# Norm and combination of the second half's first three row blocks moved ahead of the last block

## The chip, the cores and the metric

The kernel runs on one core of a Trainium2 chip. The metric is the device time of one launch in microseconds. PE is TensorE, DVE is VectorE, ACT is ScalarE, POOL is GpSimd, and SP is the engine that issues the DMAs spoken of here.

## What is computed

One decoder layer on x of 1024 rows and 1024 columns in float32: a gated recurrent branch and a sparse attention branch, merged by gates, an output projection with a residual, a norm, and a squared-ReLU MLP with a residual. The change lies between the output projection and the first products of the MLP:

```python
def rms_norm(x, g):
    xf = x.astype(jnp.float32)
    y = xf * lax.rsqrt(jnp.mean(xf * xf, axis=-1, keepdims=True) + EPS)
    return (y * g.astype(jnp.float32)).astype(x.dtype)
...
    merged = jax.nn.sigmoid(gate_a) * o_gdn + jax.nn.sigmoid(gate_b) * o_att
    x = x + merged @ w_out
    h2 = rms_norm(x, norm_mlp_g)
    x = x + jnp.square(jax.nn.relu(h2 @ w_mlp_up)) @ w_mlp_down
    return x
```

## The kernel before

**Tiles.** The 1024 rows are eight row blocks of 128 rows (qb 0 to 7). Blocks 0 to 3 are the first half, 4 to 7 the second. The attention units and the output projection `wout` go through the blocks in the order 0, 7, 1, 6, 2, 3, 5, 4, each with two units (g of 0 and 1), so block 4 is the last. Behind a block's second unit, `residual` (line 1397) adds the two PSUM banks `dd` to the residual rows x1 (the tiles w0 to w7: block 0 is in w3, 1 in w2, 2 in w6, 3 in w7, 4 in w4, 5 in w0, 6 in w5, 7 in w1), stores them by SP, and sums the squares on ACT (`th,nss<-w`). `wout` starts a block's first unit only when the residual of the block ahead has emptied both banks.

**First half.** `norm2` (line 1424) waits for the sums of squares of all four blocks, finds the inverse roots nr by a Newton iteration (`rsq_w`, line 101: with the first scaling, eleven operations of DVE on 128x4 numbers, each of which needs the one ahead of it), scales the rows on DVE and transposes them on PE into banks of two rings, `s` and `pt`, of two banks each. Each bank is evacuated by ACT (rounded part, `ha`) and then by DVE (the rest, `la`), and only then is it free again. The MLP's up-products (`dd<-ha,m`, `o<-la,m`) are computed by a scheme that multiplies sums and differences of the two halves' column halves; the first products need the first half alone.

**Second half.** `norm2b` (line 1587) waits for the sums of squares of all four blocks, makes one Newton iteration for them, scales the four blocks' second column halves (`hh<-w,nr`, y22), and passes five combinations of rows through `columns` (line 1633), one after another: set 0 (y22), set 2, set 3, set 1 and set 4. A set is sixteen transposes in four banks, with an evacuation of 128x512 by ACT (`hh`) and one by DVE (`hl`) for each bank; four operations of DVE on 128x512 (one for each block) make the rows of the next set.

**Order.** A planner (`Weave`, from line 2003) runs all these generators as chains with priorities when the program is built. It emits, at each moment of its own clock, the next step of the ready chain with the lowest number. It holds a price for each operation; a DVE operation costs 0.07 us and 1/960 us for each element of a partition. A step is what a generator emits between two `yield`s. The resulting order of each engine is fixed in the program; on the chip each engine takes its own list strictly in order and waits where an operand isn't there yet. `rsq_w` yields between its operations, so in the kernel before other operations of DVE may be emitted between them.

## Time and profile before

| | |
|---|---|
| median of 3 runs | 1824.97 us (1824.21 to 1825.02) |
| the profiled execution's own time | 1824.57 us |
| its span in the trace | 1822.9 us |
| granted TensorE clock | 1.00 |
| PE busy | 1807.4 us (99%) |
| DVE, ACT, POOL busy | 1266.2, 1036.2, 525.5 us |
| output projection ends, first MLP products begin | at about 1195 us of the span |
| the second half's sets are made | from about 1200 to 1250 us |

The times in the rows below count from the start of the span. A row of the timeline gives its start, its length, the engine, the line of the helper that records it, the operation, output and inputs, how many alike stand in it, and in brackets how long the engine was idle ahead of it and which engine it waited for. An operation's length overlaps the next one's start, so the pace of a run of operations is read from start to start. PE has next to no idle time, so the few places where it has some are what a reordering can win or lose.

### The profile page before, as it was taken

To read this page: it belongs to the slowest core of one execution; us is meant where nothing else is said; L and a number is where in the kernel's file an instruction comes from. 1 tells how busy PE (TensorE), PEld (TensorE's weight loads), DVE (VectorE), ACT (ScalarE), POOL (GpSimd) and SP (SyncE) were. 2 spreads that over 40 slices of the span, in tenths; PEclk is the share of its full clock that TensorE was granted. 3 is DMA by queue.
4 is the path that set the end of the run, shared out by engine and by line. 5 is a ranking of instruction groups with operands and counts; after the bars stand their busy time and mean duration, and the time that the engine had idled before them with its cause. 6 is when DMAs were issued, how large, how long until landed. Compare 5 with 4: busy or idle time off the path is not lost. (4 is left out here: it accounts for less than half of the span.)

```text
span 1822.9 us, 28546 instructions
## 1 busy us (share of the span) xinstructions
PE 1807.4 (99%) x10316; PEld 1542.0 (85%) x10316; DVE 1266.2 (69%) x2626; ACT 1036.2 (57%) x2273; POOL 525.5 (29%) x738
## 2 busy tenths in 40 slices
PE   9999999999999999999999999999999999999999
PEld 8999998888888888888887888887888888888887
DVE  5556768857777869764448767687766668969673
ACT  6566657765776545445337656576676664343331
POOL 0003530733461724245013111221323322222230
PEclk9999999999999999999999999999999999999999
DMA  4111242132222222231356222224535459473331
GB/s 163 48 47 47 71 128 64 49 97 76 57 58 54 78 70 62 69 84 35 98 168 208 89 77 74 73 89 149 195 136 165 147 173 347 149 249 126 102 133 55
DMA packets 192192, 198.80 MB, mean 109 GB/s; under 512 B 36737, under 2 KB 140466, under 8 KB 192050
## 3 DMA queue, kind: packets, MB, share of 16 engines
q1 hardware_dynamic: 192050, 196.97, 34.2%
q8 instruction: 81, 1.33, 0.3%
q14 instruction: 61, 0.50, 0.1%
HBM read 141.20 MB, written 55.74 MB: 108 GB/s over the span
## 5 line engine op out<-in xcount | busy, mean ns | idle before, releaser
L2114 PE MATMUL dd<-hh,w 128*128 128x512 f32 x1568 | 518.0, 402 | 0.0
L2114 PEld LDWEIGHTS dd<-hh,w 128*128 128x128 f32 x1568 | 288.2, 189 | 50.6
L2114 PE MATMUL dd<-hl,w 128*128 128x512 f32 x784 | 316.1, 403 | 0.9 <-DVE hl L2114 0.9
L2114 ACT ACTIVATE m<-m 128x512 fp32r<-128x512 f32 (+1 forms) x240 | 139.9, 625 | 80.1 <-PE o L2114 30.5
L2114 PE MATMUL dd<-w,hh 128*128 128x256 f32 x960 | 179.4, 284 | 0.4 <-DVE w L2114 0.4
L2114 PE MATMUL dd<-hh,m 128*128 128x512 f32 x520 | 172.1, 396 | 1.0 <-DVE w L2114 0.8
L2114 PEld LDWEIGHTS dd<-hl,w 128*128 128x128 f32 x784 | 147.8, 189 | 26.6 <-DVE hl L2114 1.4
L2114 DVE TENSOR_TENSOR m<-m,m 128x512 fp32r<-128x512 f32 (+2 forms) x184 | 139.4, 784 | 40.8 <-ACT m L2114 35.5
L2114 PEld LDWEIGHTS dd<-w,hh 128*128 128x128 f32 x960 | 151.5, 191 | 1.5 <-DVE w L2114 0.6
L2114 PE MATMUL dd<-w,hl 128*128 128x256 f32 x480 | 136.2, 284 | 0.0
L2114 POOL TENSOR_TENSOR sx<-sx,stmp 128x60 f32<-128x60 f32 (+24 forms) x248 | 110.1, 444 | 19.4
L2114 PEld LDWEIGHTS dd<-hh,m 128*128 128x128 f32 x520 | 96.7, 188 | 20.6 <-DVE w L2114 2.4
L2114 DVE TENSOR_SCALAR_CACHE_REDUCE tkeq<-sc,cand 128x384 f16<-128x384 f32 (+3 forms) x128 | 103.3, 807 | 1.1
L2114 POOL TENSOR_TENSOR m<-m,m 128x512 f32<-128x512 f32 x48 | 67.9, 1421 | 123.5 <-ACT m L2114 60.3
L2114 PE MATMUL dd<-hl,m 128*128 128x512 f32 x260 | 102.3, 393 | 0.9 <-POOL hl L2114 0.9
L2114 POOL TENSOR_TENSOR stmp<-sx,um 128x60 f32<-128x60 f32 (+24 forms) x186 | 79.2, 426 | 64.7 <-DMA um<-ZA 51.1
L2114 ACT ACTIVATE hh<-m 128x1024 fp32r<-128x1024 f32 x44 | 45.2, 1056 | 88.7 <-PE s L2114 41.5
L2114 ACT ACTIVATE ha<-m 128x1024 fp32r<-128x1024 f32 x44 | 45.4, 1056 | 87.7 <-PE s L2114 34.1
L2114 PEld LDWEIGHTS dd<-w,hl 128*128 128x128 f32 x480 | 91.7, 191 | 0.6
L2114 DVE TENSOR_TENSOR w<-w,w 128x1024 fp32r<-128x1024 f32 (+1 forms) x60 | 67.6, 1130 | 33.4 <-ACT w L2114 32.8
L2114 ACT ACTIVATE tkcm<-sc,cand 128x896 f16<-128x896 f32 x64 | 69.9, 1091 | 25.7 <-DVE cand L2114 22.1
L2114 PE MATMUL o<-hh,m 128*128 128x512 f32 x248 | 80.2, 391 | 0.0
(412 smaller groups left out, 4435.4 us busy)
## 6 DMA issues: line engine op xcount, KB each, us to landing
HD<-m SPq DMA_DIRECT2D x112, 256.0 KB, 2.5
m<-HD SPq DMA_DIRECT2D x56, 512.0 KB, 3.9
w<-in_w_in_dram SPq DMA_DIRECT2D x48, 512.0 KB, 3.9
m<-in_w_mlp_up_dram SPq DMA_DIRECT2D x33, 512.0 KB, 5.2
wraw<-in_w_in_dram SPq DMA_DIRECT2D x8, 1024.0 KB, 5.2
m<-in_w_mlp_down_dram SPq DMA_DIRECT2D x16, 512.0 KB, 6.8
w<-in_x_dram SPq DMA_DIRECT2D x10, 512.0 KB, 4.5
es<-GC SPq DMA_DIRECT2D x8, 512.0 KB, 4.6
```

The source lines that it names most:

```text
L2114: ins = f(*args, **kw)
```

## The change

The residuals get priority -1 instead of 1. `rsq_w` can emit a whole Newton iteration in one step (`apart=False`), and the new `roots` always does so. The first half's norm is made in two parts, blocks 0 to 2 and then block 3, each with its own Newton iteration; half of the scalings go to ACT; its priority falls from 2 to 8. For the second half a new chain `early` makes the roots of blocks 6 and 7 (one iteration) and of block 5 (another), the scaled rows and the combinations of these three blocks; `early_columns` transposes three blocks' columns of the sets 0 and 2 into three quarters of the banks and evacuates 128x384. `norm2b` is left with block 4 (a fifth iteration): `last_columns` transposes four columns of it into one bank for each of the two sets and evacuates the bank in two parts of 128x2x128. The sets 3, 1 and 4 are made for all four blocks as before. The number of matmuls and transposes is the same.

```diff
@@ -98,15 +98,19 @@
     wv = Weave(tc)
     V_, A_, G_, PE_, SY_ = (wv.engine(e, n) for e, n in ((V, "V"), (A, "A"), (G, "G"), (PE, "PE"), (SY, "SY")))
-    def rsq_w(pl, dst, src, n, tag):
-        t = pl.tile([P, n], F32, name=tag + "t")
+    def rsq_w(pl, dst, src, n, tag, apart=True):
+        t = pl.tile([P, max(n, 4)], F32, name=tag + "t")[:, :n]
         V_.tensor_scalar(dst.bitcast(I32), src.bitcast(I32), -0.5, float(0x5F3759DF), op0=OP.mult, op1=OP.add)
         for _ in range(3):
-            yield
+            if apart:
+                yield
             V_.scalar_tensor_tensor(t, dst, -0.5, src, op0=OP.mult, op1=OP.mult)
-            yield
+            if apart:
+                yield
             V_.tensor_tensor(t, t, dst, op=OP.mult)
-            yield
+            if apart:
+                yield
             V_.scalar_tensor_tensor(dst, t, 1.5, dst, op0=OP.add, op1=OP.mult)
     units = ([("misc", [(0, C_GA, 16), (16, C_IK, 72)])]
@@ -1391,7 +1395,7 @@
                         yield 0.0
             wv.done("wo", idx)
             if g:
-                wv.add(1, residual(qb, pw))
+                wv.add(-1, residual(qb, pw))
         wv.done("wout")
     def residual(qb, pw):
@@ -1420,22 +1424,31 @@
         yield
         wv.done("h2k", half, k)
+    def roots(tbs):
+        for tb in tbs:
+            yield ("ss", tb)
+        bs = slice(min(tbs), max(tbs) + 1)
+        V_.tensor_scalar(nms[:, bs], nss[:, bs], 1.0 / D, EPS, op0=OP.mult, op1=OP.add)
+        yield from rsq_w(cst, nr[:, bs], nms[:, bs], len(tbs), "n2", apart=False)
+        yield
     def norm2():
-        for tb in range(4):
-            yield ("ss", first * 4 + tb)
-        bs = slice(first * 4, first * 4 + 4)
-        V_.tensor_scalar(nms[:, bs], nss[:, bs], 1.0 / D, EPS, op0=OP.mult, op1=OP.add)
-        yield
-        yield from rsq_w(cst, nr[:, bs], nms[:, bs], 4, "n2")
-        yield
-        for tb in range(4):
-            yield ("xd", first * 4 + tb)
+        tbs = [qb for qb, g in ATT if g and qb // 4 == first]
+        for now in (tbs[:3], tbs[3:]):
+            yield from roots(now)
+            for tb in now:
+                yield ("xd", tb)
+                for c, eng in enumerate("VA"):
+                    yc = x1[tb][:, c * HALF:(c + 1) * HALF]
+                    yield eng
+                    if c:
+                        A_.activation(yc, yc, AF.Copy, scale=nr[:, tb:tb + 1])
+                    else:
+                        V_.tensor_scalar(yc, yc, nr[:, tb:tb + 1], None, op0=OP.mult)
+        yield
         for c in range(2):
             ys = [x1[first * 4 + i][:, c * HALF:(c + 1) * HALF] for i in range(4)]
-            for i in range(4):
-                V_.tensor_scalar(ys[i], ys[i], nr[:, first * 4 + i:first * 4 + i + 1], None, op0=OP.mult)
-            yield
             for k in range(4 * c, 4 * c + 4):
                 ring = (ss, ptr)[k % 2]
                 yield ring.ready
@@ -1443,6 +1456,72 @@
                 for i in range(4):
                     PE_.transpose(ps[:, i * P:(i + 1) * P], ys[i][:, (k % 4) * P:(k % 4 + 1) * P], ident)
                 wv.add(1, norm_out(first, k, ps, ring, slot_))
+            yield
+            wv.done("turned", c)
+    part = lambda h, c: [x1[4 * h + i][:, c * HALF:(c + 1) * HALF] for i in range(4)]
+    y22, comb, pairs = {}, {}, {}
+    places = {0: 0, 2: 2, 3: 4, 1: 6}
+    def early(tbs):
+        yield from roots(tbs)
+        for tb in tbs:
+            i, r = tb % 4, nr[:, tb:tb + 1]
+            b11, b12 = part(first, 0)[i], part(1 - first, 0)[i]
+            y22[i] = part(1 - first, 1)[i]
+            yield ("xd", tb)
+            yield "A"
+            A_.activation(y22[i], y22[i], AF.Copy, scale=r)
+            yield
+            yield ("turned", 0)
+            yield "V"
+            V_.scalar_tensor_tensor(b11, b12, r, b11, op0=OP.mult, op1=OP.subtract)
+            yield "V"
+            V_.scalar_tensor_tensor(b12, b12, r, y22[i], op0=OP.mult, op1=OP.subtract)
+            yield
+            wv.done("combined", i)
+    def early_columns():
+        js = [tb % 4 for tb in EARLIER]
+        for j in js:
+            yield ("combined", j)
+        yield ("wo", NA - 2)
+        for m in (0, 2):
+            if m:
+                yield
+                for j in js:
+                    yield "V"
+                    V_.tensor_tensor(y22[j], y22[j], part(first, 0)[j], op=OP.subtract)
+                yield
+            for k in range(4):
+                if k % 2 == 0:
+                    pairs[m, k // 2] = [hpair(f"{n}{places[m] + k // 2}") for n in ("hh", "hl")]
+                    for i in range(2):
+                        comb[m, k + i] = [t[:, i] for t in pairs[m, k // 2]]
+                ring = (ss, ptr)[k % 2]
+                yield ring.ready
+                ps, slot_ = ring.get()
+                for j in js:
+                    PE_.transpose(ps[:, j * P:(j + 1) * P], y22[j][:, k * P:(k + 1) * P], ident)
+                wv.add(2, early_rounded(m, k, ps, ring, slot_))
+        yield
+        wv.done("early")
+    def early_rounded(m, k, ps, ring, slot_):
+        cs = slice(min(EARLIER) % 4 * P, (max(EARLIER) % 4 + 1) * P)
+        hi, lo = (t[:, cs] for t in comb[m, k])
+        yield 0.2
+        yield "A"
+        A_.activation(hi, ps[:, cs], AF.Copy)
+        yield
+        yield "V"
+        V_.tensor_tensor(lo, ps[:, cs], hi.bitcast(F32), op=OP.subtract)
+        ring.free(slot_)
+    EARLIER = sorted(qb for qb, g in ATT[:-1] if not g and qb // 4 != first and qb != ATT[-1][0])
     wv.add(1, kprep())
     wv.add(0, loadq())
@@ -1478,7 +1557,10 @@
             h2h[2 * j + i, first], h2l[2 * j + i, first] = th[:, i, :], tl[:, i, :]
     wv.run(until=("pv", NA - 2))
-    wv.add(2, norm2())
+    wv.add(8, norm2())
+    for tbs in (EARLIER[1:], EARLIER[:1]):
+        wv.add(2, early(tbs))
+    wv.add(2, early_columns())
     NP = FF // (2 * P)
@@ -1580,55 +1662,50 @@
         if p == UP[-1]:
             wv.done("rfree", q)
-    comb = {}
     def norm2b():
-        half = 1 - first
-        for tb in range(4):
-            yield ("ss", half * 4 + tb)
-        bs = slice(half * 4, half * 4 + 4)
-        V_.tensor_scalar(nms[:, bs], nss[:, bs], 1.0 / D, EPS, op0=OP.mult, op1=OP.add)
-        yield
-        yield from rsq_w(cst, nr[:, bs], nms[:, bs], 4, "n2")
-        yield
-        yt = [hpair(n, F32) for n in ("hh6", "hh7")]
-        y22 = [yt[i // 2][:, i % 2] for i in range(4)]
-        for i in range(4):
-            tb = half * 4 + i
-            o, src, r = y22[i], x1[tb][:, HALF:], nr[:, tb:tb + 1]
-            if i % 2:
-                A_.activation(o, src, AF.Copy, scale=r)
-            else:
-                V_.tensor_scalar(o, src, r, None, op0=OP.mult)
-        wv.add(0, columns(0, y22))
-        yield
-        part = lambda h, c: [x1[4 * h + i][:, c * HALF:(c + 1) * HALF] for i in range(4)]
-        t1, t4, t3, t2 = part(first, 0), part(first, 1), part(half, 0), part(half, 1)
+        tb = ATT[-1][0]
+        i, r = tb % 4, nr[:, tb:tb + 1]
+        yield from roots([tb])
+        y = hpair("hh6", F32)[:, 0]
+        t1, t4, t3, t2 = part(first, 0), part(first, 1), part(1 - first, 0), part(1 - first, 1)
+        V_.tensor_scalar(y, t2[i], r, None, op0=OP.mult)
+        yield
+        yield ("early",)
+        wv.add(0, last_columns(0, i, y))
+        V_.scalar_tensor_tensor(t1[i], t3[i], r, t1[i], op0=OP.mult, op1=OP.subtract)
         yield ("T", 0, 3)
-        for i in range(4):
-            V_.scalar_tensor_tensor(t1[i], t3[i], nr[:, half * 4 + i:half * 4 + i + 1], t1[i], op0=OP.mult, op1=OP.subtract)
-        yield
-        for i in range(4):
-            V_.tensor_tensor(t2[i], y22[i], t1[i], op=OP.subtract)
-        yield
-        wv.add(0, columns(2, t2))
-        yield ("col", 2)
-        for i in range(4):
-            V_.scalar_tensor_tensor(t3[i], t3[i], nr[:, half * 4 + i:half * 4 + i + 1], y22[i], op0=OP.mult, op1=OP.subtract)
-        yield
+        V_.tensor_tensor(t2[i], y, t1[i], op=OP.subtract)
+        yield
+        wv.add(0, last_columns(2, i, t2[i]))
+        V_.scalar_tensor_tensor(t3[i], t3[i], r, y, op0=OP.mult, op1=OP.subtract)
+        yield ("T", 2, 3)
         wv.add(1, columns(3, t3))
         yield "V"
-        for i in range(4):
-            V_.tensor_tensor(t4[i], t4[i], t2[i], op=OP.subtract)
+        for j in range(4):
+            V_.tensor_tensor(t4[j], t4[j], t2[j], op=OP.subtract)
         yield ("col", 3)
         wv.add(1, columns(1, t1))
         yield ("col", 1)
         wv.add(1, columns(4, t4))
-    places = {0: 0, 2: 2, 3: 4, 1: 6}
+    def last_columns(m, i, row):
+        yield ss.ready
+        ps, slot_ = ss.get()
+        for k in range(4):
+            PE_.transpose(ps[:, k * P:(k + 1) * P], row[:, k * P:(k + 1) * P], ident)
+        yield
+        for kk in range(2):
+            src = ps[:, kk * 2 * P:(kk + 1) * 2 * P].rearrange("p (a b) -> p a b", a=2)
+            hi, lo = (t[:, :, i * P:(i + 1) * P] for t in pairs[m, kk])
+            A_.activation(hi, src, AF.Copy)
+            yield
+            V_.tensor_tensor(lo, src, hi.bitcast(F32), op=OP.subtract)
+            if kk:
+                ss.free(slot_)
+            yield
+            wv.done("T", m, 2 * kk)
+            wv.done("T", m, 2 * kk + 1)
     def columns(m, rows):
         yield
@@ -1646,7 +1723,7 @@
                 th, tl = (hpair(f"{n}{places[m] + k // 2}") for n in ("hh", "hl"))
                 for i in range(2):
                     comb[m, k + i] = th[:, i], tl[:, i]
-            wv.add(0 if m in (0, 2) else 3, rounded(m, k, ps, ring, slot_))
+            wv.add(3, rounded(m, k, ps, ring, slot_))
         wv.done("col", m)
     def rounded(m, k, ps, ring, slot_):
```

The first place is DVE between the residual of block 3 (w_11479) and the last attention unit's softmax. `mx` and `nm` are the softmax's maximum and sum, `pl` a part of its transposed weights, `nss` the sums of squares, `nms`, `nr` and `n2t` the numbers of a Newton iteration. Before:

```order
L2114 TENSOR_TENSOR w_11479<-w_11479,dd 128x512 x2
L2114 TENSOR_TENSOR sg<-o,sg 128x512
L2114 TENSOR_SCALAR nm<-mx 128x1
L2114 RECIPROCAL mx<-nm 128x1
L2114 TENSOR_TENSOR pl<-pt,ph 128x512 x2
L2114 TENSOR_SCALAR nms<-nss 128x4
```

Now:

```order
L2191 TENSOR_SCALAR nm<-mx 128x1
L2191 TENSOR_SCALAR nms<-nss 128x2
L2191 TENSOR_SCALAR nr<-nms 128x2
...
L2191 SCALAR_TENSOR_TENSOR nr<-n2t,nr 128x2
L2191 TENSOR_SCALAR nms<-nss 128x3
L2191 TENSOR_SCALAR nr<-nms 128x3
...
L2191 SCALAR_TENSOR_TENSOR nr<-n2t,nr 128x3
L2191 RECIPROCAL mx<-nm 128x1
L2191 TENSOR_SCALAR w_11216<-w_11216,nr 128x512
```

Two whole iterations, of eleven operations each, now stand between `nm` and the RECIPROCAL that is the next to be waited for by the softmax.

The second place is PE where set 0's last transposes stand, behind the first MLP products (`dd<-ha,m`, `o<-ha,m`). Before, `hh_13823` and `hh_13824` are the scaled rows of all four blocks:

```order
L2114 MATMUL dd<-la_13352,m_13731 128x512
L2114 MATMUL dd<-ha_13351,m_13731 128x512
L2114 MATMUL o<-ha_13345,m_13742 128x512
L2114 MATMUL o<-la_13346,m_13742 128x512
L2114 MATMUL o<-ha_13345,m_13742 128x512
L2114 MATMUL s<-ident,hh_13823 128x128 x2
L2114 MATMUL s<-ident,hh_13824 128x128 x2
L2114 MATMUL pt<-ident,hh_13823 128x128 x2
L2114 MATMUL pt<-ident,hh_13824 128x128 x2
```

Now, `hh_13826` is block 4's scaled rows alone:

```order
L2191 MATMUL o<-ha_13347,m_13691 128x512
L2191 MATMUL o<-ha_13349,m_13721 128x512
L2191 MATMUL o<-la_13350,m_13721 128x512
L2191 MATMUL s<-ident,hh_13826 128x128 x4
L2191 MATMUL o<-ha_13349,m_13721 128x512 x2
L2191 MATMUL o<-la_13350,m_13721 128x512
```

Four transposes stand where sixteen stood, and the other twelve have moved up, in threes, ahead of the end of the output projection.

The third place is DVE ahead of these four transposes, whose bank is freed by the row `hl_13792<-s`; `hh_13826` is written there too, and the rows `m` prepare weights and sums of the products. Before, the scaling of y22 had this ahead of it:

```order
L2114 SCALAR_TENSOR_TENSOR nr<-n2t,nr 128x4
L2114 TENSOR_TENSOR m_13797<-m_13797,dd 128x512
L2114 TENSOR_SCALAR hh_13823<-w_11554,nr 128x512
L2114 TENSOR_SCALAR hh_13824<-w_11359,nr 128x512
L2114 TENSOR_TENSOR m_13816<-m_13575,m_13816 128x512
```

Now:

```order
L2191 SCALAR_TENSOR_TENSOR nr<-n2t,nr 128x1
L2191 TENSOR_SCALAR hh_13826<-w_11554,nr 128x512
L2191 TENSOR_TENSOR m_13747<-m_13624,m_13747 128x512
L2191 TENSOR_TENSOR m_13767<-m_13767,dd 128x512
L2191 SCALAR_TENSOR_TENSOR w_11216<-w_11554,nr,w_11216 128x512
L2191 TENSOR_TENSOR m_13815<-m_13625,m_13815 128x512
L2191 TENSOR_TENSOR m_13831<-m_13628,m_13831 128x512
L2191 TENSOR_TENSOR hl_13792<-s,hh_13791 128x384
```

An evacuation of set 2's early part has come to stand between block 4's scaling and the transposes, behind five other operations.

## Rows read from the trace of the kernel before

**Rows 1.** The page's first part: span, and busy time of each engine.

```profile
span 1822.9 us, 28546 instructions
PE 1807.4 (99%) x10316; PEld 1542.0 (85%) x10316; DVE 1266.2 (69%) x2626; ACT 1036.2 (57%) x2273; POOL 525.5 (29%) x738
```

**Rows 2.** Timeline of PE at four stalls, with the row ahead of each.

```profile
1179.84 0.39 PE L2114 MATMUL dd<-hh,m 128*128 128x512 f32 x1
1181.06 0.50 PE L2114 MATMUL dd<-hh,m 128*128 128x512 f32 x1 [0.83 <-DVE w L2114]
...
1212.89 0.39 PE L2114 MATMUL o<-ha,m 128*128 128x512 f32 x1
1213.87 1.07 PE L2114 MATMUL s<-ident,hh 128*128 128x128 f32 x4 [0.59 <-DVE hh L2114]
...
1231.69 0.40 PE L2114 MATMUL o<-hh,m 128*128 128x512 f32 x1
1232.95 0.66 PE L2114 MATMUL pt<-ident,w 128*128 128x128 f32 x4 [0.86 <-DVE hl L2114]
...
1238.32 0.40 PE L2114 MATMUL o<-hh,m 128*128 128x512 f32 x1
1238.56 0.39 PE L2114 MATMUL dd<-hh,m 128*128 128x512 f32 x1
1240.19 0.63 PE L2114 MATMUL s<-ident,w 128*128 128x128 f32 x4 [1.24 <-DVE hl L2114]
```

**Rows 3.** Waits of PE from 1260 us: engine, waited for, sum, times, longest.

```profile
PE pt L2114 <- DVE hl L2114: 0.2, 1, 0.2
```

**Rows 4.** Timeline of PE at the last attention unit's transposes.

```profile
1166.57 1.11 PE L2114 MATMUL pt<-ident,pr 128*128 128x128 f32 x8
1167.43 0.70 PE L2114 MATMUL dd<-hh,m 128*128 128x512 f32 x2
```

**Rows 5.** Timeline of DVE around the last attention unit's softmax.

```profile
1164.31 0.20 DVE L2114 TENSOR_SCALAR nm<-mx 128x1 f32<-128x1 f32 x1
1165.83 0.17 DVE L2114 RECIPROCAL mx<-nm 128x1 f32<-128x1 f32 x1 [1.31 <-ACT pr L2114]
```

**Rows 6.** Timeline of ACT at the scaling by that reciprocal.

```profile
1166.03 0.83 ACT L2114 ACTIVATE pr<-pr,mx 128x640 f32<-128x640 f32 x1 [0.23 <-DVE mx L2114]
```

**Rows 7.** Timeline of DVE in norm2's Newton iteration: paced, and beside POOL.

```profile
1173.93 1.15 DVE L2114 SCALAR_TENSOR_TENSOR nr<-n2t,nr 128x4 f32<-128x4 f32 x1
...
1177.60 0.15 DVE L2114 TENSOR_TENSOR n2t<-n2t,nr 128x4 f32<-128x4 f32 x1
...
1178.18 0.16 DVE L2114 TENSOR_TENSOR n2t<-n2t,nr 128x4 f32<-128x4 f32 x1
```

**Rows 8.** Timeline of POOL: an addition at the softmax, one at norm2's iteration.

```profile
1164.55 1.30 POOL L2114 TENSOR_TENSOR sg<-sg,m 128x512 f32<-128x512 f32 x1
...
1173.77 1.29 POOL L2114 TENSOR_TENSOR m<-sg,m 128x512 fp32r<-128x512 f32 x1 [0.18 <-ACT m L2114]
```

**Rows 9.** Timeline of ACT: scalings of weights, a sum of squares, two evacuations.

```profile
1168.25 1.70 ACT L2114 ACTIVATE m<-m,vecs 128x256 f32<-128x256 f32 x4
...
1197.00 1.27 ACT L2114 ACTIVATE m<-m,vecs 128x128 f32<-128x128 f32 x4
1198.17 1.04 ACT L2114 ACTIVATE th<-w 128x1024 bf16<-128x1024 f32 x1
...
1215.47 0.59 ACT L2114 ACTIVATE hh<-pt 128x512 fp32r<-128x512 f32 x1
1215.94 0.60 ACT L2114 ACTIVATE hh<-s 128x512 fp32r<-128x512 f32 x1
```

**Rows 10.** Timeline of DVE: norm2b's iteration from first to last, and later operations.

```profile
1200.95 0.16 DVE L2114 TENSOR_SCALAR nms<-nss 128x4 f32<-128x4 f32 x1
...
1211.68 0.16 DVE L2114 SCALAR_TENSOR_TENSOR nr<-n2t,nr 128x4 f32<-128x4 f32 x1
...
1213.24 0.88 DVE L2114 TENSOR_SCALAR hh<-w,nr 128x512 f32<-128x512 f32 x2
...
1218.00 2.73 DVE L2114 SCALAR_TENSOR_TENSOR w<-w,nr,w 128x512 f32<-128x512 f32 x4
...
1229.81 2.49 DVE L2114 TENSOR_TENSOR w<-w,w 128x512 f32<-128x512 f32 x4
```

More of the change, by code (lines that the diff above doesn't have):

```diff
@@ new lines, in norm2b @@
+        tb = ATT[-1][0]
[4 more added lines that the diff above has]
+        V_.tensor_scalar(y, t2[i], r, None, op0=OP.mult)
+        yield
+        yield ("early",)
+        wv.add(0, last_columns(0, i, y))
+        V_.scalar_tensor_tensor(t1[i], t3[i], r, t1[i], op0=OP.mult, op1=OP.subtract)
+        yield ("T", 0, 3)
+        V_.tensor_tensor(t2[i], y, t1[i], op=OP.subtract)
```

1 line of the change is left out of this document (removed).

## The prediction

> **What bounds the kernel now.** I read the page's first part first: PE is busy 1807.4 of 1822.9 us, 99% [rows 1], so whatever a reordering wins must come out of PE's idle time, and whatever it loses shows there as a new wait. Then I read PE's timeline from 1160 to 1260 us, the stretch that the change reaches. Four stalls stand there [rows 2]. Measured from start to start, less a step of 0.23 us (1179.84 is a plain step; 1238.32 to 1238.56 is one, too), they are 1181.06 - 1179.84 - 0.23 = 0.99 us (the residual of block 5 has to empty the banks), 1213.87 - 1212.89 - 0.23 = 0.75 (set 0's transposes wait for the scaled rows), 1232.95 - 1231.69 - 0.23 = 1.03 and 1240.19 - 1238.56 - 0.23 = 1.40 (transposes wait for a bank that DVE has still to evacuate). In all 4.17 us, or 0.23% of the time: that is the most that the change can win. Last I looked at what follows: from 1260 us to the end PE waits 0.2 us in a single place [rows 3]. So there is no slack behind the stretch that could swallow a shift, and each microsecond won or lost before 1260 reaches the end in full. All rows below are of one profiled execution of 1824.57 us, 0.40 under the median; I add the 0.40 at the end.
>
> **What the change leaves alone.** The transposes of sets 0 and 2 are 32 in either kernel, and no matmul comes or goes, so PE's work is the same. What changes is who waits for whom. DVE gets 33 more operations on a few numbers (five Newton iterations of eleven instead of two), and ACT takes some scalings over from DVE. Where these lie beside other work they cost nothing; the places below are those where somebody waits. The residuals of blocks 1, 6 and 2 come a little earlier than before, behind attention work that has no stall there; I take 0.
>
> **Step 1, the softmax of the last attention unit.** Before, DVE makes `nm` at 1164.31, is idle 1.31 us, and makes the RECIPROCAL at 1165.83, as soon as ACT's exponentials have ended [rows 5]. ACT scales by it from 1166.03 for 0.83 us, to 1166.86 [rows 6], and PE's transposes of the result stand in the group from 1166.57 [rows 4]: the fourth of them needs ACT, at 1166.57 + 3 x 0.11 = 1166.9, and gets it in time. Now two whole iterations, 22 operations, stand ahead of the RECIPROCAL, in that idle place. How long do they take? In norm2's iteration the small operations start 0.195 us apart: from 1177.60 to 1178.18 there are three steps [rows 7]. On 128x2 or 128x3 numbers I take the same, since their 0.15 us can't be four elements' work. From 1164.51 that is 22 x 0.195 = 4.3 us, to 1168.8. One thing more: POOL's addition runs from 1164.55 for 1.30 us, to 1165.85 [rows 8]. A small operation of DVE that started at 1173.93 beside such an addition (1173.77, 1.29 us) took 1.15 us and ended with it, at 1175.08 [rows 7, 8]. So I let the third operation, the first with two inputs, end at 1165.87 instead of 1165.1; 19 are left, 3.7 us, to 1169.6; then the RECIPROCAL, 0.17, the hand-over to ACT, 0.2, and ACT's 0.83: 1170.8. PE's order has two matmuls more ahead of the transposes now, so it would come there at 1166.9 + 2 x 0.23 = 1167.36. The stall is 3.4 us; without the hold by POOL it is 2.6. I take 3.3. The same pattern comes once more: block 3's own iteration, 2.15 us in one piece, now stands ahead of the last `pl<-pt,ph`, and PE's matmul on it comes within half a microsecond of that; with a hold by POOL it costs up to 0.9, without it nothing. So this step is +2.6 to +4.3.
>
> The Trainium skill has two rules on this. The page SBUF — State Buffer, in "Who interferes with whom", says that a DVE instruction with two SBUF inputs and a GpSimd instruction that reads SBUF exclude each other, the later one waiting for the whole of the first: by it the third operation waits until POOL is done, and the stall is 3.4 us; the row with 1.15 us agrees. The page Perfetto Trace Analysis, in "Optimizing Scalar/DVE Operations", gives about 60 ns as the time that a DVE instruction on SBUF keeps the engine: by it the 22 operations are, as an estimate, 1.3 us, they fit the gap, and the stall is nothing. The 0.195 us from start to start speaks against it here, since each operation needs the result of the one ahead; what it would make of the whole is the first rival.
>
> **Step 2, the residual of block 5** (0.99 us before). Its two additions on DVE now stand behind five `la` evacuations of the first half's transposes, which have moved up ahead of it, and PE goes through these transposes faster than DVE evacuates: a group of four is 4 x 0.11 = 0.43 us, an evacuation some 0.62 (1229.81: 2.49 us for four like it [rows 10]). Over the eight groups that is 8 x 0.19 = 1.5 us, less the four banks' head start, with 1.3 us of additions among them. I get 1.2 us of waits in place of 0.99: +0.2, with -0.1 to +0.8 as ends.
>
> **Step 3, block 4's four transposes** (0.75 us before). They wait for a bank of ring `s`, and by PE's order that is the one that holds an early part of set 2; it is free after ACT's `hh<-s` and DVE's `hl_13792<-s`. I follow the chain from the end of block 5's residual. On DVE: three `la` and one `m` at 0.62, two combinations at 0.68 (1218.00: 2.73 us for four [rows 10]), 3.8; the iteration for block 5, 11 x 0.195 = 2.15. Then ACT, where the list is full: block 5's scaling 0.6; three weight scalings of 1.70 and two roundings of 0.47 (1215.47 to 1215.94), 6.0; four evacuations, at most 0.47 each, 1.9; block 4's sum of squares 1.04; two roundings 0.94; 1.70 and 1.27 of scalings; two roundings 0.94; 1.27; the evacuation 0.47 [rows 9]. Last DVE's 0.62. That is 3.8 + 2.15 + 0.6 + 6.0 + 1.9 + 1.04 + 0.94 + 2.97 + 0.94 + 1.27 + 0.47 + 0.62 = 22.7 us. PE has 83 matmuls of 0.23 and 24 transposes of 0.11 in the same stretch: 21.7. So PE waits 1.0 us with nothing in the way, and 2.2 with one hold by POOL of 1.2 in the iteration; with two, or with block 4's iteration late by itself (2.15 us, behind the sum of squares, and five operations before the evacuation), 3.5. I take 2.3, +1.55, with +0.25 to +2.75 as ends. What is gained is plain too: norm2b's iteration took from 1200.95 to 1211.68 with other work between its operations, and the four scalings came at 1213.24 [rows 10]; that now concerns one block. But the bank that the four transposes need hangs on the list of ACT and DVE, and not on the iteration alone.
>
> **Step 4, the later banks** (1.03 + 1.40 us before). The sets 3, 1 and 4 are still made for all four blocks, and four `w<-w,w` of 2.49 us [rows 10] still stand as one piece ahead of an evacuation that frees a bank, which is the pattern at 1229.81 that held PE at 1231.69. Shifts of half an evacuation decide how much of each is left. I take 2.6 in place of 2.43, +0.2; the ends are -2.4 (both gone) and +2.5 (each doubled).
>
> **Sum.** 3.3 + 0.2 + 1.55 + 0.2 = 5.25 us; 1824.57 + 5.25 + 0.40 = **1830.2 us**. The low ends give 2.6 - 0.1 + 0.25 - 2.4 = +0.35, 1825.3; the high ends 4.3 + 0.8 + 2.75 + 2.5 = +10.35, 1835.3.
>
> **The rivals.**
>
> *The iterations are hidden (faster).* If an operation keeps DVE for some 0.07 us, as the planner's price has it, 22 of them take 1.5 us, from 1164.5 to 1166.0, the RECIPROCAL is 0.2 late, and the early combinations do what they can: only four transposes of sets 0 and 2 are left behind the last block, and the waits for the rows and for the banks go. With all 4.17 us gone it is 1824.97 - 4.17 = 1820.8; if the residual's 0.99 stays, 1821.8. It decides at a pace of about 0.08 us for a small operation. For it: the gap of 1.31 us before the RECIPROCAL is there [rows 5]. Against it: the pace of 0.195 in the trace [rows 7].
>
> *Paid and given back (no change).* The softmax waits 2.6 us, but the later evacuations find DVE free, since the combinations of three blocks are done early, and both bank stalls go: the low ends above, 1825.3, anything from 1822 to 1828.5. For it: a PE that comes 3 us later gives ACT and DVE time to clear their lists. Against it: ACT's list of 22.7 us runs from the residual, and moves with it.
>
> *POOL holds every iteration (slower still).* POOL's additions of 1.30 us come often in this stretch, and each of the five iterations can meet one or two, at 1.2 us a time. Three of the iterations lie on the way to PE: the high ends, about 1834.5.
>
> That the change doesn't do what it says I rule out but for one point: the order has the twelve transposes of set 0 ahead of the end of the output projection, but the bank of block 4's four waits for later work than the iteration; that is step 3.
>
> **How the numbers follow.** The forecast (1828.6 to 1832) gets 0.45: step 1 is read from rows and adds to the time by itself, steps 3 and 4 are long sums with a small difference. No change gets 0.28, the faster case 0.15 (0.02 of it above the bound), POOL's 0.12. A measurement of this kernel can tell about 0.2%, 3.65 us, from no change: below 1821.3 is faster, above 1828.6 slower. So faster has 0.13, the same 0.28 + 0.02 = 0.30, slower 0.45 + 0.12 = 0.57. The range leaves out the faster case and the upper half of POOL's: 1822.0 to 1834.5.
>
> **What would show it.** Step 1: a wait of PE's `pt<-ident,pr` for ACT of about 3 us at 1167, and 22 small operations of DVE in a row between `nm` and RECIPROCAL, 0.195 apart, the third long; if the RECIPROCAL comes before 1166.5 the step is wrong and with it the forecast. Step 2: waits of PE for `la` and for `w` of 1.2 in all. Step 3: `s<-ident,hh` waiting for DVE by 1 to 3.5 us, and ACT without idle time ahead of it. Step 4: waits for `hl` of 1.5 to 5 us in the 30 us behind that. The forecast falls if the waits between 1160 and 1260 us sum up to less than 6 us.

## The result, and the profile after

| | before | changed |
|---|---|---|
| median of 5 runs | 1824.65 us (1823.88 to 1825.02) | 1833.98 us (1833.17 to 1835.31) |
| ratio to before | | 1.0054, 95% interval 1.0042 to 1.0067 |
| span of the profiled execution | 1822.9 us | 1832.6 us |
| granted TensorE clock, mean | 1.00 | 0.997 |
| PE busy | 1807.4 us | 1812.0 us |

The change makes the kernel 9.3 us slower by these medians; as a ratio of the runs it is 0.54%. The time lies 0.5 us inside the upper end of the predicted range, and the ratio just above that end (1834.5 / 1824.97 = 1.0052); the shift is nearly twice the 5.25 us of the forecast. The page of the changed kernel answers to [rows 1] with

```profile
span 1832.6 us, 28593 instructions
PE 1812.0 (99%) x10316; PEld 1545.2 (84%) x10316; DVE 1275.0 (70%) x2658; ACT 1039.2 (57%) x2282; POOL 526.6 (29%) x738
```

PE has the same 10316 instructions as before and is busy 4.6 us longer. So not all of the loss is waiting: a part of it is the same work, done more slowly. What PE waits for between 1160 and 1260 us is the following (engine, waited for, sum in us, times, longest):

```profile
PE s L2191 <- DVE hl L2191: 4.5, 3, 3.2
PE pt L2191 <- ACT pr L2191: 3.1, 1, 3.1
PE pt L2191 <- DVE hl L2191: 0.9, 2, 0.6
PE dd L2191 <- DVE w L2191: 0.5, 1, 0.5
```

That is 9.0 us, where the four stalls of [rows 2] have 3.52 us of idle time. Two waits of over 3 us are new. The timeline of PE at the first, the softmax of the last attention unit, beside [rows 4], and at the second, block 4's four transposes:

```profile
1166.96 0.49 PE L2191 MATMUL pt<-ident,pr 128*128 128x128 f32 x3
1170.57 1.33 PE L2191 MATMUL pt<-ident,pr 128*128 128x128 f32 x5 [3.12 <-ACT pr L2191]
...
1211.82 0.39 PE L2191 MATMUL o<-la,m 128*128 128x512 f32 x1
1215.41 1.09 PE L2191 MATMUL s<-ident,hh 128*128 128x128 f32 x4 [3.21 <-DVE hl L2191]
1216.15 1.20 PE L2191 MATMUL o<-ha,m 128*128 128x512 f32 x2
1217.15 0.63 PE L2191 MATMUL o<-la,m 128*128 128x512 f32 x1
1217.58 0.63 PE L2191 MATMUL o<-ha,m 128*128 128x512 f32 x1
```

The last two rows start 0.43 us apart, where a matmul of this shape takes a step of 0.23 us elsewhere. Stretches of 1 us show why; behind the busy times and counts stand the granted clock, the share of the DMA engines and GB/s:

```profile
1169.00:1170.00 1.00, 0.00 (x0) 0.00 (x0) 0.91 (x5) 0.32 (x1) 0.00 (x0) 1.00 0.02 8
...
1171.00:1172.00 1.00, 1.00 (x6) 1.00 (x5) 0.00 (x0) 1.00 (x4) 0.00 (x0) 0.50 0.00 0
1172.00:1173.00 1.00, 1.00 (x4) 0.71 (x4) 0.00 (x0) 1.00 (x3) 0.00 (x0) 0.50 0.00 0
...
1217.00:1218.00 1.00, 1.00 (x3) 0.72 (x3) 0.38 (x1) 1.00 (x3) 0.00 (x0) 0.50 0.06 16
...
1220.00:1221.00 1.00, 1.00 (x4) 0.71 (x4) 0.19 (x1) 0.14 (x1) 0.00 (x0) 0.50 0.00 0
```

Behind each of the two long waits the granted clock is 0.50, the lower of its two levels, 1.2 instead of 2.4 GHz, for some 3 us of PE's work the first time and 6 us the second; then it is 1.00 again. Taken from start to start, as the excess over the usual step, this costs 1.57 us behind the first wait and 2.88 us behind the second. The waits themselves are 3.28 and 3.37 us by the same measure. The rest of the stretch has hardly changed: the residual of block 5 costs 0.70 us (0.99 in [rows 2]), and four bank waits together 0.95 + 0.48 + 0.73 + 0.63 = 2.79 us (2.43). With block 5's residual that is 14.6 us of excess, against 4.2 in [rows 2]; the 10.4 us between them are somewhat more than the 9.7 by which the span grew.

DVE, ACT and the transposes at the first wait, beside [rows 5] and [rows 6]:

```profile
1164.22 0.20 DVE L2191 TENSOR_SCALAR nm<-mx 128x1 f32<-128x1 f32 x1
1164.34 0.17 DVE L2191 TENSOR_SCALAR nms<-nss 128x2 f32<-128x2 f32 x1
1164.55 1.22 DVE L2191 TENSOR_SCALAR nr<-nms 128x2 int32<-128x2 int32 x1
...
1169.41 0.16 DVE L2191 SCALAR_TENSOR_TENSOR nr<-n2t,nr 128x3 f32<-128x3 f32 x1
1169.49 0.16 DVE L2191 RECIPROCAL mx<-nm 128x1 f32<-128x1 f32 x1
```

```profile
1169.68 0.83 ACT L2191 ACTIVATE pr<-pr,mx 128x640 f32<-128x640 f32 x1 [1.40 <-DVE mx L2191]
```

Twenty-two small operations stand between `nm` and RECIPROCAL. From the third on, those that need the result of the one ahead start 0.195 us behind it, and the one beside POOL's addition took 1.22 us. The RECIPROCAL, which needs none of them, starts 0.08 us behind the last. It comes 3.7 us later than before, and ACT and PE with it.

At the second wait, DVE from the first operation of block 4's iteration to the evacuation that frees the bank:

```profile
1207.41 0.14 DVE L2191 TENSOR_SCALAR nms<-nss 128x1 f32<-128x1 f32 x1
...
1208.55 1.19 DVE L2191 TENSOR_TENSOR n2t<-n2t,nr 128x1 f32<-128x1 f32 x1
...
1210.55 0.49 DVE L2191 TENSOR_SCALAR hh<-w,nr 128x512 f32<-128x512 f32 x1
...
1212.15 1.44 DVE L2191 SCALAR_TENSOR_TENSOR w<-w,nr,w 128x512 f32<-128x512 f32 x1
...
1214.72 0.54 DVE L2191 TENSOR_TENSOR hl<-s,hh 128x384 fp32r<-128x384 f32 x1
```

Block 4's scaled rows are there at 1211.04. The iteration in one piece took 3.1 us, with one hold of 1.19 beside an addition of POOL, and five operations follow the scaling before the evacuation starts at 1214.72; PE starts 0.15 us after its end.

### The profile page after: what moved, and what is told of

Read it like the earlier page. It is cut to its first block, busy times and chain, and to the rows that moved or that the text cites. A ratio compares the mean times of both kernels' runs of the same rounds, so it can differ in the third digit from the quotient of the medians.

```text
span 1832.6 us, 28593 instructions
## 1 busy us (share of the span) xinstructions
PE 1812.0 (99%) x10316; PEld 1545.2 (84%) x10316; DVE 1275.0 (70%) x2658; ACT 1039.2 (57%) x2282; POOL 526.6 (29%) x738
## 4 chain that ended last, share of the span: by engine, by line
PE 94%; DVE 3%; ACT 1%; issue 1%; POOL 1%; POOLq 0%; ACTq 0%; DVEq 0%
PE dd L2191 55%; PE o L2191 15%; PE s L2191 7%; PE pt L2191 6%; PE tt L2191 4%; PE cc L2191 2%; PE sq L2191 2%; PE jj L2191 2%; PE oo L2191 1%; DVE w L2191 1%; DVE hl L2191 0%; DVE m L2191 0%; PE tp L2191 0%; POOL hl L2191 0%; DVE pr L2191 0%
## 5 line engine op out<-in xcount | busy, mean ns | idle before, releaser
L2191 ACT ACTIVATE m<-m 128x512 f32<-128x512 f32 (+1 forms) x240 | 139.8, 625 | 79.5 <-PE dd L2191 33.3
L2191 DVE TENSOR_TENSOR m<-m,m 128x512 fp32r<-128x512 f32 (+2 forms) x184 | 143.1, 803 | 38.3 <-ACT m L2191 32.9
```

What stands on the lines that cost most here:

```text
L2191: ins = f(*args, **kw)
```

## The experiments

The theory was that the Newton iterations in one piece cost the time; that the small operations are priced too low by the planner is its other half. The rivals were that moving the combinations or the residuals ahead costs it, and, for the second wait, that the evacuation of the bank does. All ratios are to the kernel before, run beside it.

**The iterations held until the softmax (e1_hold).** The order behind them is planned anew.

```diff
     def roots(tbs):
+        yield ("p", NA - 1, 3)
         for tb in tbs:
```

> The changed kernel with one line more: every Newton iteration of the second norm is held until the last attention unit's softmax has been issued, so that the RECIPROCAL comes ahead of all of them. Theory (the 22 small operations ahead of the RECIPROCAL made PE wait 3.1 us, and the half clock behind that wait cost 1.6 us more): that wait and the half clock behind it are gone, 4.7 us less than the changed kernel, about 1829.3 us if the wait of block 4's transposes (3.2 us and 2.9 us of half clock) stays. Rival (PE's wait there has another cause, ACT's scalings ahead of it): within 1 us of the changed kernel, 1834. If block 4's wait falls below 2 us as well by the new order and the clock stays whole: 1823 to 1825.

Measured: 1827.27 us, ratio 1.0017 (1.0008 to 1.0025). The wait for ACT's scaling is gone, and so is the one for block 4's rows; others take a part of their place:

```profile
PE pt L2192 <- DVE la L2192: 1.9, 1, 1.9
PE o L2192 <- DVE pl L2192: 1.0, 1, 1.0
PE dd L2192 <- DVE w L2192: 0.9, 2, 0.8
PE s L2192 <- DVE nms L2192: 0.7, 1, 0.7
```

A half clock follows the longest of these, 1.9 us, which ends at 1190.67; it lasts from 1191 to 1195 us:

```profile
1192.00:1193.00 1.00, 1.00 (x4) 0.80 (x3) 1.00 (x3) 1.00 (x3) 0.00 (x0) 0.50 1.04 346
```

Both waits went, but the clock did not stay whole, and the time lies between the 1829.3 and the 1823 to 1825 that were expected. Of the 9.3 us, 2.9 are left, so most of the loss hangs on where the pieces stand. That both waits went says that the second one isn't independent of the first, or of the plan around it.

**The softmax's wait alone (e2_chain22, e3_chain11).** The kernel before got 22, or 11, small operations with unused results ahead of the last RECIPROCAL, entered behind the planner's back, so that no other instruction moves.

```diff
         yield
+        if idx == NA - 1 and i == 3:
+            kept = dict(wv.busy), wv.t
+            t = cst.tile([P, 4], F32, name="jt")[:, :3]
+            V_.tensor_tensor(t, nss[:, 0:3], nss[:, 0:3], op=OP.max)
+            for _ in range(21):
+                V_.tensor_tensor(t, t, nss[:, 0:3], op=OP.max)
+            wv.busy, wv.t = kept
         V_.reciprocal(mx[:, 0:1], nm[:, 1:2])
```

> The kernel before, with 22 additional dependent operations of DVE on 128x3 between the exponentials and the last RECIPROCAL, their results unused, everything else in the same order. Theory: at 0.195 us each and held by POOL's addition until 1165.85, they end at 1169.9, ACT's scaling ends at 1171.1, PE waits 4.1 us at 1166.9 and then runs at half clock for some 3 us, which costs 1.6 us: 5.7 us more than before, 1830.4. Rival A (small operations cost 0.07 us each): 1.5 us of work in a gap of 1.3 us, within 0.5 us of before. Rival B (the half clock in the changed kernel has nothing to do with the wait): 4.1 us more, clock 1.00, 1828.8.

> As the run with 22, with 11 operations. Theory: the first is held until 1165.85, the eleventh ends at 1167.8, ACT's scaling at 1169.0, PE waits 2.0 us. If the half clock follows only waits as long as the two in the changed kernel (3.1 and 3.2 us), the clock stays at 1.00 and the kernel takes 2.0 us more than before, 1826.7; if it follows this wait as well, some 3.5 us more, 1828.2. Rival A (0.07 us each): no difference to before.

Measured: 1841.63 us (1.0093) and 1838.52 us (1.0075). Both are far above every theory, and PE's waits don't account for it: with 11 operations it waits 1.5 us there. The difference is spread: from some 300 us on a 128x512 step is longer by 3 to 5 ns, between 1300 and 1500 us it takes 232 ns instead of 227, and behind about 1500 us it is the same again. The edit had a side effect, a tile more. The same operations were therefore written into nms, which is free at that point, and the tile alone was tried as well.

**The same without a new tile (e5_chain22n, e6_chain11n).** `t = nms[:, 0:3]` in place of the tile.

> The kernel before with the 22 additional operations ahead of the last RECIPROCAL, written into nms instead of a tile of their own, so that every address stays as it was (the tile of the earlier runs with 11 and 22 operations moved all that lies behind it by 32 bytes, and PE's matmul step of 128x512 was 232 ns instead of 227 ns there). Theory: PE waits 4.1 us for ACT's scaling and runs at half clock for some 3 us behind it, 1.6 us: 5.7 us more than before, 1830.1. Rival A (the operations cost DVE 0.07 us each): within 0.5 us of before. Rival B (the half clock isn't a consequence of the wait): 4.1 us, 1828.4.

> The same with 11 operations. Theory: they end at 1167.8, PE waits 2.0 us, and since the clock stayed at 1.00 behind a wait of 1.5 us in the earlier run with 11, it does so here: 1826.4. If the clock falls behind this wait: some 1828.

Measured: 1830.34 us, ratio 1.0031 (1.0018 to 1.0045), and 1826.21 us, ratio 1.0011 (1.0002 to 1.0020). The wait of PE, with 22 and then with 11:

```profile
PE pt L2121 <- ACT pr L2121: 3.7, 1, 3.7
```

```profile
PE pt L2121 <- ACT pr L2121: 1.6, 1, 1.6
```

and the two stretches at and behind it, in the same order (PE, PEld, DVE, ACT and POOL busy, granted clock, DMA share, GB/s):

```profile
1166.00:1171.00 5.00, 1.37 (x8) 0.92 (x6) 3.47 (x22) 0.91 (x3) 0.16 (x1) 0.88 0.71 227
1171.00:1176.00 5.00, 4.92 (x14) 4.10 (x15) 2.13 (x5) 4.15 (x10) 0.00 (x0) 0.50 0.00 0
```

```profile
1166.00:1171.00 5.00, 3.44 (x20) 2.68 (x19) 2.14 (x9) 3.60 (x8) 0.00 (x0) 1.00 0.48 160
1171.00:1176.00 5.00, 5.00 (x28) 4.22 (x27) 3.45 (x7) 3.61 (x8) 2.60 (x3) 1.00 0.00 0
```

This settles the first wait. Eleven operations cost about the wait they make, 2.0 us, and the clock stays whole. Twenty-two cost 6.2 us: 3.9 of wait and, with the clock at 0.50, 14 matmuls in the next 5 us instead of 28. The half clock is the wait's consequence, for these two kernels differ in the number of the operations alone, and so in the wait's length. It doesn't come in every execution: of the five runs with 22 operations, four took 1830.2 to 1832.0 us at a mean clock of 0.998 to 0.999, and one took 1826.84 us at 1.000. That run has no trace, so how long PE waited in it is not known.

**A tile that nobody reads (e8_pad).**

```diff
     nss, nms, nr = (cst.tile([P, NB], F32, name=n) for n in ("nss", "nms", "nr"))
+    pad = cst.tile([P, 4], F32, name="pad")
+    V.memset(pad, 0.0)
```

> The kernel before with a small tile more that nobody reads, 32 bytes of each partition, in the pool that lies lowest; all tiles of the left side's pools move by 32 bytes, those of the right side's stay. If the pace of PE's matmuls hangs on the addresses: 232 ns for a 128x512 step and some 13 us more, 1837. If the earlier runs with 11 and 22 operations were slow for another reason: 1824.5.

Measured: 1837.26 us, ratio 1.0073. It explains the two odd runs; e2_chain22 and e5_chain22n, too, differ in nothing but the tile. A hundred microseconds in which PE never waits, before and with the tile:

```profile
1300.00:1400.00 100.00, 100.00 (x442) 82.80 (x442) 65.25 (x97) 68.24 (x135) 32.34 (x24) 1.00 0.46 154
```

```profile
1300.00:1400.00 100.00, 100.00 (x432) 80.82 (x431) 64.21 (x96) 67.74 (x132) 28.72 (x20) 1.00 0.46 156
```

**The residuals alone (e4_residual).** `wv.add(-1, residual(qb, pw))` in the kernel before.

> The kernel before with one part of the change alone, the residuals at priority -1. Theory: PE's order around the attention shifts, no wait comes or goes: within 0.5 us of before, 1824.2 to 1825.2. Rival (the residuals ahead of the softmax's work cost attention time): 1 us or more slower, with waits of PE between 1060 and 1165 us.

Measured: 1824.18 us, ratio 0.9999 (0.9990 to 1.0008). That part of the change costs nothing.

**The iterations' operations one by one (e7_apart, e9_apart_same).** `apart=False` is taken out of `roots`, and each iteration gets a temporary of its own, since they overlap now: four more tiles in the first kernel, slices of one 32-byte tile in the second.

> The changed kernel with the operations of each Newton iteration emitted one by one again, as in the kernel before (a tile of its own for each iteration, in sizes that leave the addresses at the same offset from a multiple of 64 bytes). Six small operations stand ahead of the RECIPROCAL instead of 22. Theory (the piece of 22 is what held the softmax): PE's wait there falls from 3.1 to 0.5 us and the clock stays whole behind it, 4.2 us less; with block 4's iteration spread, the order behind it is another one; 1826 to 1830 if one wait with half clock is left, 1822 to 1825 if none. Rival (the combinations and scalings moved ahead cost the time, not the pieces): 1832 or more.

> The run with the iterations' operations emitted one by one, again, with the five iterations' temporaries in one 32-byte tile, so that every address is the one of the kernel before. The earlier run of this order had a matmul step of 232 instead of 227 ns (its tiles lay 128 bytes higher), which the run with the unread tile prices at 13.1 us. Theory: the step is 227 ns again, PE doesn't wait at the softmax, block 4's transposes wait 1 to 3 us with half clock behind them: 1836.3 - 13.1 = 1823.2. Rival (that run was slow by its order): 1834 or more.

Measured: 1836.26 us (1.0068), with a step of 232 ns again, and 1825.83 us, ratio 1.0009 (1.0001 to 1.0018), with 227. The expectation for the second, 1823.2, was 2.6 us too low, but the rival is out: one by one, with every combination still moved ahead, the loss is 1.6 us instead of 9.3. PE doesn't wait at the softmax. In the second kernel it waits 1.3 us for the bank of block 4's transposes and then 0.5 and 0.7 us for the evacuations of these, in short order, and half clock follows these three together:

```profile
1225.00:1226.00 1.00, 1.00 (x3) 0.81 (x3) 0.95 (x3) 0.02 (x1) 0.00 (x0) 0.50 0.47 176
```


**Early evacuations first (e12_evac).** `wv.add(0, early_rounded(...))` in place of 2, in the changed kernel, so that the evacuation of block 4's bank comes soon behind its scaling.

> The changed kernel as it is (whole iterations in one piece), with the early evacuations at priority 0 alone. On DVE the one that frees block 4's bank then stands two operations behind block 4's scaling instead of six. Theory: the softmax's wait of 3.1 us and its half clock stay, block 4's wait falls from 3.2 to about 1 us and the half clock behind it (2.9 us) doesn't come: 1829. Rival (the half clock comes by something else at that place): 1832 or more.

Measured: 1833.81 us, ratio 1.0052 (1.0039 to 1.0066), the wait 3.3 us. The theory's number fell, but the run doesn't settle whether the evacuation's place makes the wait, for two other things changed with it. PE comes to the transposes 0.9 us earlier, and POOL's additions hold block 4's iteration twice instead of once:

```profile
1208.91 1.20 DVE L2191 TENSOR_TENSOR n2t<-n2t,nr 128x1 f32<-128x1 f32 x1
...
1210.34 1.15 DVE L2191 SCALAR_TENSOR_TENSOR n2t<-nr,nms 128x1 f32<-128x1 f32 x1
...
1213.91 1.01 DVE L2191 TENSOR_TENSOR hl<-s,hh 128x384 fp32r<-128x384 f32 x2
```

The iteration ends 1.4 us later than in the changed kernel. The evacuation starts 2.0 us behind that end here, and 4.2 us behind it there.


**What makes the second wait (e13_last, e14_price).** In the first, block 4's iteration alone is emitted one by one; in the second, all five stay in one piece, and the planner's price of an operation of DVE on fewer than four numbers is the measured one, with nothing added behind it.

```diff
-        yield from rsq_w(cst, nr[:, bs], nms[:, bs], len(tbs), "n2", apart=False)
+        yield from rsq_w(cst, nr[:, bs], nms[:, bs], len(tbs), "n2", apart=tbs == [ATT[-1][0]])
```

```diff
-                return wv.issue(name, ins, 0.07 + n / 960, 0.12, self.port(op, args, kw))
+                small = wv.shared and n < 4
+                return wv.issue(name, ins, 0.195 if small else 0.07 + n / 960, 0 if small else 0.12, self.port(op, args, kw))
```

> The changed kernel with block 4's iteration alone emitted one by one, the other four in one piece. The softmax's wait (3.1 us and 1.6 us of half clock) stays in either case. Theory A (block 4's wait of 3.2 us comes from its iteration in one piece, which the planner takes for 0.8 us and which took 3.0 us with a hold by POOL): the wait falls to 1 us or less, without half clock: 1828.5 to 1830. Theory B (it comes from the planner's clock having run ahead of the chip by then, by the four earlier pieces): the wait stays above 2.5 us and the time at 1832 to 1834.5.

> The changed kernel with the planner's price of a DVE operation on fewer than 4 numbers, from the shared stage on, at the measured 0.195 us instead of 0.07. The planner still emits each piece as it stands, and the 22 operations stay ahead of the RECIPROCAL, so the softmax's wait and its half clock stay (4.7 us). Theory B (the planner's clock ran ahead): with the right price PE's list has block 4's transposes where they can run, the wait there falls below 1.5 us and its half clock goes: 1828 to 1830. Theory A (the piece itself): no less than 1832.

Measured: 1826.22 us, ratio 1.0011 (1.0002 to 1.0020), and 1826.66 us, 1.0012 (1.0003 to 1.0021). Both are faster than expected. In the first the softmax's wait is as it was, and block 4's is 0.6 us:

```profile
PE pt L2191 <- ACT pr L2191: 3.2, 1, 3.2
PE s L2191 <- DVE hh L2191: 0.6, 1, 0.6
PE dd L2191 <- DVE w L2191: 0.5, 1, 0.5
```

Not because the iteration is faster. On DVE it ends at 1217.48 there, with other work between its operations, and in the changed kernel at 1210.35:

```profile
1217.48 0.15 DVE L2191 SCALAR_TENSOR_TENSOR nr<-n2t,nr 128x1 f32<-128x1 f32 x1
```

```profile
1210.35 0.16 DVE L2191 SCALAR_TENSOR_TENSOR nr<-n2t,nr 128x1 f32<-128x1 f32 x1
```

It is later, and PE hardly waits, because the planner knew: emitted one by one, each operation carries the 0.12 us after which the planner lets the next one follow, and PE's list has the transposes 29 instructions later than in the changed kernel. The second kernel shows the same at the softmax, where the wait was expected to stay. DVE has the same 22 operations and the RECIPROCAL at 1169.60, but PE has 13 instructions more ahead of the transposes and waits 0.31 us:

```profile
1169.97 0.49 PE L2191 MATMUL pt<-ident,pr 128*128 128x128 f32 x3
1170.77 0.44 PE L2191 MATMUL pt<-ident,pr 128*128 128x128 f32 x2 [0.31 <-ACT pr L2191]
```

At block 4's transposes it waits 1.5 us for the bank, and the clock stays at 1.00. Theory B as it stands is out: in e13_last the four earlier pieces stay, and the wait goes. What both edits change is how long the planner takes a piece to be: the piece hides its own length from it, eleven operations of 0.07 for 0.195 us each, and PE's fixed list sends it to transposes whose rows or bank aren't there. Either edit replans DVE's list as well, and no run changed PE's list alone, so for the second wait this account is the likeliest one, not shown step by step.

**What the change is worth without that (e10, e11, e15).** To the one-by-one kernel of e9_apart_same were added: the early evacuations at priority 0; or set 2's early part held back until block 4 has completed set 0; or both.

```diff
             if m:
-                yield
+                yield ("T", 0, 3)
```

> As the run before it, and the evacuations of the three early blocks at priority 0 instead of 2, so that on DVE they come ahead of the weights' and sums' operations. Theory (block 4's transposes wait for the bank that these evacuations free): that wait falls below 1 us, no half clock behind it, 2 to 3 us less than without: 1820.5 to 1822. Rival (the wait is for block 4's own scaling): no difference.

> As the run with one-by-one iterations, and set 2's early part held back until block 4 has completed set 0, so that block 4's four transposes of set 0 wait for none of its banks. Theory: the wait ahead of set 0's last transposes is gone, and one ahead of set 2's takes its place, since twelve more transposes and their evacuations then stand behind the output projection: 1821 to 1825. If holding back costs nothing: 1820.

> The one-by-one iterations with set 2's early part held back and the early evacuations at priority 0, the two edits that each took the loss away. Theory (the early combination, without pieces, gains no more than what it costs in new waits for the same banks): within 1 us of the kernel before, 1823.2 to 1825.2. If the two edits add up: 1821 to 1822.5, faster than before.

Measured: 1824.07 us (1.0001, 0.9992 to 1.0010), 1824.46 us (1.0001, 0.9992 to 1.0010) and 1821.81 us, ratio 0.9985 (0.9975 to 0.9994). The first edit's theory was wrong: block 4's wait grew to 2.6 us. No half clock follows it, and the time is 1.8 us below that of e9_apart_same. The second lies in its range, 1821 to 1825. Both together do more than my theory for them said: this kernel is 0.15% faster than the one before. Its waits from 1060 us to 1262 us are

```profile
PE pt L2202 <- DVE hl L2202: 0.8, 1, 0.8
PE dd L2202 <- DVE w L2202: 0.4, 1, 0.4
PE s L2202 <- DVE nms L2202: 0.3, 1, 0.3
```

PE comes to block 4's transposes without a wait, and only one bank wait is left of [rows 2]. The change's idea is sound, then; the 2.8 us gained lie within the bound of 4.17 us, worked out from those rows.

## Why the prediction was right or wrong

**What bounds the kernel.** Right. The 9.7 us by which the span grew arose between 1160 and 1250 us, and behind that next to nothing was swallowed (the wait of 0.2 us in [rows 3] is gone). The list of stalls leaves out one wait of 0.19 us at 1196 us.

**Step 1.** Right in mechanism and size: 22 operations 0.195 us apart, one hold by POOL, RECIPROCAL at 1169.49 where the working says 1169.6, a wait of 3.28 us for 3.3. Two details were wrong. The working counts the RECIPROCAL's 0.17 us twice, since the 0.2 us to ACT already runs from its start (1165.83 to 1166.03 in [rows 5, 6]). I let the third operation be held, as the first with two inputs; it was the second, `nr<-nms`, 1.22 us, with one. The page SBUF — State Buffer of the Trainium skill, in "Who interferes with whom", counts a tensor_scalar among the instructions that can contend, which this row bears out. The second half of the step, up to 0.9 us at block 3's iteration, didn't come.

**The missing term.** This is the step that failed: the sum prices a wait at its own length and puts the clock behind it at nothing, without a reason. Behind the two long waits PE ran at half clock, and that cost 1.57 + 2.88 = 4.45 us. The waits themselves, 3.28 + 0.70 + 3.37 + 2.79 = 10.14 us, are 5.97 more than the 4.17 of before, where the sum has 5.25; so the missing term makes up nearly all of the error. Nothing in the trace of before showed it, since its longest wait is one of 1.56 us, far ahead of the stretch, and its clock is 1.00 behind it, too:

```profile
146.77 0.50 PE L2114 MATMUL sq<-ikh,iqt 128*128 128x512 f32 x1 [1.56 <-ACT iqt L2114]
```

But steps 1 and 3 forecast waits longer than any of its rows, and I priced them as if the rows reached that far. There is a page on it: TensorE: Matmul & The Clock Gate of the Trainium skill, in "Why this matters for your kernels", warns of idle gaps between matmuls for just that reason. The rows of the two long waits here agree with it. By it the forecast would have had a second term at least behind the 3.3 us of step 1.

**Step 2.** Right that little changes; 0.70 us instead of the 1.2 I took, below the 0.99 of before.

**Step 3.** The term was too small, 3.37 us of wait for 2.3, within its ends, and its account was wrong in part: I followed the bank's evacuation through ACT's list to 2.3, and named block 4's late iteration with five operations behind it only for the end at 3.5. The rows show that end: the iteration with one hold, then five operations, then the evacuation. Behind it, as far as e13_last and e14_price show, stands that the lists were made with a price that is a third of what the iteration takes. The last sentence of that step, that the bank hangs on the lists "and not on the iteration alone", led me past the iteration.

**Step 4.** 2.79 us for 2.6, as said: the pattern stays.

**The rivals.** The faster case rested on the small operations' price of 0.07 us. It is refuted for a chain: where each operation needs the one ahead, the pace is 0.195 us. Where it needs none, as the RECIPROCAL behind the last of the 22, it follows by 0.08 us, near the price. The planner prices a chain in one piece at 0.07 us an operation, and that is the root of the first long wait and the likeliest one of the second. I named this price in one rival and didn't draw the consequence for PE's list, which the same planner had made. "Paid and given back" did not happen in the changed kernel, though it did in e13_last: the softmax's wait is paid there with its half clock, both bank stalls are gone, and the time is 1826.22. POOL's holds came in three of the five iterations (1.22, 0.88 and 1.19 us) and made up a part of the waits; that the measured 1833.98 is near this rival's 1834.5, and so still within the range, is luck, for half of the way there is the clock, which no rival has.

What stays open is how much of the second wait each piece before it contributes. e1_hold and e13_last both remove it, by different edits, and each replans what lies between. Open, too, is what the evacuation's place on DVE costs by itself.

## What to carry to other kernels

Where a planner fixes each engine's order, its prices are part of the program: a chain of small dependent operations that is priced by its elements sends the other engines to work that isn't ready. Emit such a chain in steps that carry its latency, or give it its measured price, here 0.195 us for each operation that needs the one ahead. And a forecast wait that is longer than any in the trace needs a second term, the clock behind it; count what PE will idle in one stretch, and look whether a row shows the clock after a wait of that length.

## What the runs showed of the hardware

The clock: at waits of 3.1, 3.2 and 3.7 us the granted clock fell to 0.50, for some 3 to 7 us; in e5_chain22n it fell while PE still waited. After one wait of 1.6 us (e6_chain11n) it stayed at 1.00, and in e10_apart_evac also after one of 2.6:

```profile
1205.00:1215.00 10.00, 7.38 (x39) 5.93 (x37) 9.97 (x19) 8.52 (x20) 3.62 (x3) 1.00 0.07 27
1215.00:1225.00 10.00, 9.99 (x47) 8.32 (x48) 8.12 (x12) 4.74 (x10) 3.42 (x3) 1.00 0.14 52
```

But in e1_hold it fell behind one of 1.9 us, with waits of 0.3 and 0.7 us shortly ahead of it, and in e9_apart_same behind three shorter waits in a row. So one wait's length isn't the whole of it.

Small operations of DVE: in a chain, each needing the one ahead, they start 0.195 us apart on 128x1 to 128x4 numbers; one that needs none of them follows by 0.08 us (1169.41 to 1169.49 in the changed kernel).

The addresses: a tile of 32 bytes in each partition, that nobody reads, shifts the tiles of one side of the memory against those of the other, and between 1300 and 1500 us a matmul step goes from 227 to 232 ns; the kernel takes 13.1 us more, some 8 of them ahead of that stretch. A shift by 128 bytes did the same in e7_apart. The kernels timed here whose tiles kept their addresses have 227 ns. That the addresses do it, and not the tile in another way, is concluded from this; why they would, no run tells. It means that an experiment which adds so much as a scratch tile has to be compared with a kernel that has the same tile, or put its data where nothing moves.
